# Reordering the pool gate and the key norm inside the mixer of a macaron block

## The chip, the cores and the metric

The kernel runs on one core of a Trainium2 chip. The metric is the device time of one execution in microseconds, and the figure given for a kernel is the median of several runs. For the kernel before, that is 2142.58 us over three runs (2141.94 to 2145.56).

Five engines take part: TensorE (PE) multiplies matrices, VectorE (DVE), ScalarE (ACT) and GpSimd (POOL) do the elementwise work, and SyncE (SP) issues most of the transfers from memory. Each engine works through its own list of instructions in order, and waits on semaphores where it needs what another engine or a transfer makes.

## The reference

The block takes 256 tokens of width 2048 in float32 through a feed-forward part, a mixer and a second feed-forward part (width 5632). The change lies in the mixer alone:

```python
def _hybrid_mixer(u, w_in, ...):
    p = u @ w_in
    z_a, z_b, g_a, g_b = jnp.split(p, IN_SPLITS, axis=-1)   # 3360, 1024, 2048, 2048
    y_a = _rwkv7_branch(z_a, ...) @ w_proj_a
    y_b = _pool_branch(z_b, pool_w, pool_scale) @ w_proj_b
    m = jax.nn.sigmoid(g_a) * y_a + jax.nn.sigmoid(g_b) * y_b
    return m @ w_out

def _rwkv7_branch(z, mu, w0, w2, a0, a2, g2, k_k, k_a, r_k, gn_w, gn_b):
    zs = zf + (_token_shift(zf) - zf) * mu.astype(f32)
    r, k, v, lw, la, lg = jnp.split(zs, RWKV_SPLITS, axis=-1)
    w = -jax.nn.softplus(-(w0.astype(f32) + jnp.tanh(lw) @ w2.astype(f32))) - 0.5
    decay = jnp.exp(-jnp.exp(w))
    a = jax.nn.sigmoid(a0.astype(f32) + la @ a2.astype(f32))
    ...
    kk = hv(k * k_k.astype(f32))
    kk = kk / jnp.maximum(jnp.sqrt(jnp.sum(kk * kk, axis=-1, keepdims=True)), L2_EPS)
    k = k * (1.0 + (a - 1.0) * k_a.astype(f32))
    y = _wkv7_scan(r_h, hv(decay), k_h, v_h, -kk, kk * a_h)
    ...

def _pool_branch(z, pool_w, pool_scale):
    ...                       # per group of 256 columns: mean over the last 2, 4, 8, 16
    mixed = pooled - zf       # tokens, less the token itself
    y = jnp.einsum('bsgc,gcd->bsgd', mixed, pool_w.astype(jnp.float32))
    y = y.reshape(bsz, seq, POOL_WIDTH) * pool_scale.astype(jnp.float32)
```

So a gate multiplies each branch's projection; the pool branch has four groups with a small matrix each (256 by 256), and the recurrent branch needs, per head of 64 columns, the norm of the scaled keys k times k_k.

## The kernel before, in words

**How float32 is multiplied.** Each matrix is held as a high and a low half. A 512 KB piece of weights is loaded into a buffer `w32` (4 of them), ACT copies its high half to `wH` (line 101) and DVE subtracts that to get `wL` (line 102), 5 buffers each. TensorE then does three matmuls per product: high by high, high by low, low by high (`mm3`, or the inner loop of `ch_g`). Nearly all of PE's work is of this kind, and each piece of weights is used once.

**Two shapes of projection.** `tok_g` has tokens on the partitions and 512 output columns: one weight load of four k steps, 24 matmuls of 512 columns. `ch_g` has channels on the partitions: matmuls of 256 columns (line 204). Both are generators: after each three matmuls they yield the time that these are reckoned to take (MM and MC, 0.2265 and 0.12 us each), and on the last one they emit the evacuation of the accumulators.

**The order of the work.** The order of PE's instructions inside the mixer is written out by hand (`manual_schedule`, line 570); the other engines' lists are made by a scheduler that orders ready instructions by priority, where the weight splits and the evacuations of projections get a boost. The hand-made order is:

1. the small projection for decay, a and g (`ch_g`, 288 columns);
2. `z_g(0)`: k, v and r of the first half of the heads, each shifted by one token in `shift`;
3. `p_g`: for each of the four pool groups, the projection `pool_window` (line 587) and, one group late, its mix `pool_mix` (line 621). DVE makes the window sums (3 dependent steps or more per half, line 601 and on) and ACT and DVE split them into `mxT` (lines 616 and 617). The mix of the last group follows directly behind the mix of the third;
4. the recurrent branch, `rwkv` (line 637), for the first and then the second half of the heads. It is a chain of steps with little PE work, and `weave` (line 563) fills the gaps: each `yield 8` in `rwkv` means that 8 us worth of matmuls of the generator `rest()` are put there before the chain goes on. `rest()` (line 551) runs, in order, the pool's projections with their gates, `b_g(0)` to `b_g(2)`; `z_g(1)`, which the second half needs; `b_g(3)`; the four gates `ga_g` of the recurrent branch; and the first part of its projection.

`b_g(c)` computes 512 columns of the pool gate (a `tok_g` over w_in with a sigmoid, into `sgb`) and then the pool's projection (a `tok_g` over w_proj_b, whose operands are the four mixes' results `yb`, listed in `pT`), multiplies the two on DVE, and stores the product to memory through POOL's queue (line 514). The gate for c = 0 was made ahead of the whole mixer (`sgb0`).

**The chain of one half in `rwkv`.** Fifteen registers `R` of 128 by 1024 are made once and shared by both halves; a register's next use waits for its last readers. The steps up to the first products:

- 4 us of fill; the low-rank matmuls `lora` for the decay and for a (16 matmuls), with sigmoids on ACT into registers 0 and 2;
- the running sums of the decay on DVE (16 scans, line 690) into register 4, and the two exponentials on ACT (lines 694 and 695) into 0 and 1;
- v copied with its halves exchanged (register 10), and transposed on PE in two parts, 3 us of fill ahead of each (`pV`, line 718), evacuated by ACT;
- `kk`, four scalings of k on ACT (line 729, register 3), and their square `sq` on ACT (line 730, register 4); 3 us of fill; the norm, 16 small matmuls into `pn` (line 735);
- DVE's lower bound `n1`, the power -0.5 on POOL (`n2`, line 740), and DVE's copy `nb` to 64 columns per head (line 742, register 4 again); 8 us of fill;
- 8 transposes of `nb` into `pk` (line 750), which DVE multiplies into `kk`;
- `k2`, four activations on ACT (line 757) and a DVE multiply (register 5), then the scaled operands `BK` and `AR` on DVE (lines 764 to 787);
- 16 us of fill, the products `pA` (line 800), and further the solve on DVE (lines 837 to 855) with 42 us of fill until `pM` (line 866), the state's recurrence over four chunks, and the output.

The evacuations into PSUM banks go by two pools of four banks: `mm` and `mc` of the projections share one, all the chain's small products share the other.

Of the kernel before, what the change touches and what calls it, by code (L numbers as in the profile page):

```python
# [11 lines left out]
AF = mybir.ActivationFunctionType  # L12
ALU = mybir.AluOpType
# [3 lines left out]
P = 128  # L17
D = 2048
S = 256
DFF = 5632  # L20
NKD = D // P
# [24 lines left out]
class Block:  # L46
# [380 lines left out]
    def mixer(s, prm, uT, rs, resid, emit, gpost, reload):  # L427
        nc = s.nc
        w_in = prm["w_in"]
        at = s.T_at(uT)  # L430
        s.rsb = s.const([P, S], "rsb")

        sgb0 = s.unit((P, 2, 512), F32, "sgb0")

        def ev_sig(dst):
            def ev(h, ps):
                nc.scalar.activation(out=dst(h), in_=ps, func=AF.Sigmoid, scale=rs[h])
            return ev
        GA, GB = RCOLS + W, RCOLS + W + D
        s.gemm_tok(w_in, GB, at, NKD, ev_sig(lambda h: sgb0[:, h]), lead=True)  # L440

        for h in range(2):
            t = s.tmp("rb")
            nc.vector.tensor_copy(t[:, :P], rs[h].to_broadcast([P, P]))
            ps = s.psum("rb")
# [37 lines left out]
        z = [{}, {}]  # L483

        def z_g(hf):
            for nme, zc in (("k", 1), ("v", 2), ("r", 0)):
                z[hf][nme] = s.unit((P, 4, S), F32, "z" + nme)
                for b in range(2):
                    c0 = zc * W + hf * 512 + b * 256

                    def ev_z(banks):
                        s.shift(banks[0], P, c0 // P,
                                [z[hf][nme][:, b * 2 + i] for i in range(2)])
                    yield from s.ch_g(w_in, c0, 256, at, NKD, ev_z, 8)
# [7 lines left out]
            return pT[k // 2][0][:, k % 2], pT[k // 2][1][:, k % 2]  # L502
        msp = s.dp.tile([4, P, 2, 512], F32, tag="msp", name="msp")

        def b_g(c):
            if c == 0:
                sg = [sgb0[:, 0], sgb0[:, 1]]
            else:
                sg = [s.tmp("sgb"), s.tmp("sgb")]
                yield from s.tok_g(w_in, GB + c * 512, at, NKD, ev_sig(lambda h: sg[h]))  # L510

            def ev_pb(h, ps):
                nc.vector.tensor_tensor(out=sg[h], in0=ps, in1=sg[h], op=ALU.mult)
                nc.gpsimd.dma_start(out=msp[c, :, h], in_=sg[h])
            yield from s.tok_g(prm["w_proj_b"], c * 512, at_b, NKW, ev_pb)

        def p_g():
            mix = None
            for g, win in enumerate(POOL_WINDOWS):
                mxT = s.unit((P, 2, 2, S), F32R, "mxT")  # L520
                yield from s.pool_window(g, win, at, w_in, mxT)
                if g:
                    yield from s.pool_mix(g - 1, mix, prm["pool_w"], pT)
                mix = mxT
            yield from s.pool_mix(3, mix, prm["pool_w"], pT)

        sga = []
# [21 lines left out]
        pair = s.pair_g(prm["w_proj_a"], (0, 512), at_a, NKW, 4, (ev_pa(0), ev_pa(1)))  # L549

        def rest():
            for c in range(3):
                yield from b_g(c)
            yield from z_g(1)
            yield from b_g(3)
            for c in range(4):
                yield from ga_g(c)
            for t in pair:
                if t is None:
                    return  # L560
                yield t
# [8 lines left out]
        with s.tc.manual_schedule(engines={mybir.EngineType.PE}):  # L570
            for _ in s.ch_g(w_in, 3 * W, 288, at, NKD, ev_l, 4):
                pass
            for g in (z_g(0), p_g()):
                for _ in g:
                    pass
            fill = rest()
            for hf in range(2):
                weave(chain(hf), fill)
            for _ in fill:
                pass  # L580
# [56 lines left out]
    def rwkv(s, hf, z, lz, prm, yH, yL):  # L637
        nc = s.nc
        V, A, G, T = nc.vector, nc.scalar, nc.gpsimd, nc.tensor
        col = lambda nme, i: s.col[nme][:, hf * 4 + i:hf * 4 + i + 1]  # L640
# [4 lines left out]
        def reg(n, *shape):  # L645
            t = s.R[n]
            if len(shape) == 2:
                return t.rearrange("p (a b) -> p a b", a=shape[0])
            if len(shape) == 3:
                return t.rearrange("p (a b c) -> p a b c", a=shape[0], b=shape[1])  # L650
            if len(shape) == 4:
                return t.rearrange("p (a b c d) -> p a b c d", a=shape[0], b=shape[1],
                                   c=shape[2])
            return t
        ch = lambda t: t.rearrange("p i (c t) -> p i c t", c=NCH)
        fl = lambda t: t.rearrange("p i t -> p (i t)")
# [9 lines left out]
        def lora(ps, n, q):  # L666
            for i in range(2):
                o = cs(2 * q + i)
                T.matmul(ps[:, i], lwH[:, n, o], lz[n], start=True, stop=False)
                T.matmul(ps[:, i], lwL[:, n, o], lz[n], start=False, stop=True)  # L670
        sw = reg(0, 4, S)
        yield 4
        for q in range(2):
            ps = s.psum("pw").rearrange("p (i t) -> p i t", i=2)
# [4 lines left out]
        a = reg(2, 4, S)  # L679
        for q in range(2):  # L680
            ps = s.psum("pa").rearrange("p (i t) -> p i t", i=2)
# [21 lines left out]
        Xd = s.R[4][:, :512].rearrange("p (t g) -> p t g", g=16)  # L703
        Xo = s.R[4][:, 512:].rearrange("p (g t) -> p g t", g=16)
        BKt = [reg(1, *t5), reg(2, *t5)]

        k, v = z["k"], z["v"]
        vs = reg(10, 4, S)
        vp = lambda t: t.rearrange("p i (a b t) -> p (i a) b t", a=2, b=2)
        for b in range(2):  # L710
# [1 line left out]
        for pr in range(2):  # L712
            yield 3
            pss = []
            for src in (v, vs):
                ps = s.psum("pV").rearrange("p (i c) -> p i c", i=4)
# [3 lines left out]
            for b in range(2):  # L720
                c = 2 * pr + b
                pe, po = pss[1 - b], pss[b]
                A.copy(EVs[O, :, c], pe[O, :, :64])
                A.copy(ODs[E, :, c], po[E, :, 64:])

        kk = reg(3, 4, S)
        sq = reg(4, 4, S)
        for i in range(4):
            A.activation(out=kk[:, i], in_=k[:, i], func=AF.Copy, scale=col("k_k", i))
        A.activation(out=fl(sq), in_=fl(kk), func=AF.Square)  # L730
        yield 3
        ps = s.psum("pn")
        for i in range(4):
            for h in range(2):
                T.matmul(ps[:, h * 8 + 2 * i:h * 8 + 2 * i + 2], sq[:, i, h * P:h * P + P],
                         s.bones[:, 0:P:64], start=True, stop=True)
        n1 = s.small(16, "n1", bufs=1)
        V.tensor_scalar(out=n1, in0=ps[:, :16], scalar1=1e-24, scalar2=None, op0=ALU.max)
        n2 = s.small(16, "n2", bufs=1)
        G.tensor_tensor(out=n2, in0=n1, in1=s.mhalf, op=ALU.pow)  # L740
        nb = reg(4, 16, 64)
        V.tensor_copy(nb, n2.unsqueeze(2).to_broadcast([P, 16, 64]))
        nbf = nb.rearrange("p a b -> p (a b)")
        yield 8
        for q in range(2):
            ps = s.psum("pk").rearrange("p (i t) -> p i t", i=2)
            for i in range(2):
                for h in range(2):
# [3 lines left out]
                            op=ALU.mult)  # L752
# [11 lines left out]
        for i in range(4):  # L764
            V.scalar_tensor_tensor(out=qb[:, i], in0=r[:, i], scalar=col("r_k", i),
                                   in1=k2[:, i], op0=ALU.mult, op1=ALU.mult)
# [24 lines left out]
        for q in range(2):  # L791
            ar, bk = AR[q], BK[q]
            for i in range(2):
                g4 = slice(8 * q + 4 * i, 8 * q + 4 * i + 4)
                yield ((16, 0), (3, 4))[q][i]
                pAs = [s.psum("pA").rearrange("p (c j t) -> p c j t", c=NCH, j=2)
                       for _ in range(2)]
                for c in range(NCH):
                    for h, R in ((0, E), (1, O)):
                        T.matmul(pAs[h][:, c], bk[R, i, c], ar[h][R, i, c], start=True,  # L800
                                 stop=True)
                for h, R, RK in ((0, E, O), (1, O, E)):
                    ps = pAs[h]
                    for o in (0, 32):
                        A.copy(Xd[h * 64 + o:h * 64 + o + 32, :, g4]
                               .rearrange("p t g -> p g t"),
                               ps[h * 64 + o:h * 64 + o + 32, :, 0, o:o + 32])
                    A.copy(Xo[h * 64:h * 64 + 32, g4], ps[h * 64:h * 64 + 32, :, 0, 32:])
                    V.tensor_tensor(out=Xrb[R, g4], in0=ps[R, :, 1],
                                    in1=mb[R, :, 1].to_broadcast([64, NCH, C]), op=ALU.mult)  # L810
                    V.tensor_tensor(out=ar[h][RK, i], in0=ps[RK],
                                    in1=mb[RK].to_broadcast([64, NCH, 2, C]), op=ALU.mult)
            yield (5, 4)[q]
            pBs = [s.psum("pB").rearrange("p (i c t) -> p i c t", i=2, c=NCH)
                   for _ in range(2)]
            for i in range(2):
                for c in range(NCH):
                    for h, R in ((0, E), (1, O)):
                        T.transpose(pBs[h][:, i, c],
                                    bk[R, i, c].rearrange("p j t -> p (j t)"),  # L820
                                    s.ident[R, R])
            for h in range(2):
                A.copy(BKt[q][:, :, :, h], pBs[h])
# [35 lines left out]
            A.copy(tt[R, :, o:o + 32], td[R])  # L859
        for h in range(2):  # L860
            G.memset(tt[h * 64 + 32:h * 64 + 64, :, :32], 0.0)
        yield 42
        ps = s.psum("pM").rearrange("p (g t) -> p g t", g=16)
        for g in range(16):
            for h in range(2):
# [95 lines left out]
        for q in range(2):  # L961
            pg = pgs[q]
# [114 lines left out]
```

## Time and profile before

| what | value |
| --- | --- |
| median of three runs | 2142.58 us |
| the profiled execution | 2143.21 us, of which the span is 2141.5 |
| PE busy | 2101.6 us, 11077 matmuls |
| DVE, ACT, POOL busy | 1258.7, 1116.1, 78.1 us |
| memory | 406.99 MB moved, mean 190 GB/s |
| weight splits on DVE (`wL`) | 734, 884.4 us, 1212 ns each |
| weight splits on ACT (`wH`) | 734, 760.1 us, 1042 ns each |
| granted clock of PE over the span | 0.991 |
| PE's share of the chain that ended last | 95% |

The profile comes from one execution. An engine's busy time is what its instructions took; its idle time is put down to what released the instruction that came next. The groups of instructions are listed by line of the kernel, engine and operands; for 128x1024 pieces the splits are the largest groups on DVE and ACT. PE's matmuls overlap in its pipeline, so the mean duration of one (392 ns for 512 columns) is longer than the step from one start to the next. The granted clock is the share of full speed at which PE was allowed to run in a stretch of time; a stage that waited may also show a lower clock behind the wait. The names on the left of an arrow are what is written, those on the right what is read.

### The profile page before, as it was taken

What the parts mean: (1) busy time and instruction counts of PE and PEld (TensorE: products, weight loads), DVE (VectorE), ACT (ScalarE), POOL (GpSimd) and SP (SyncE); (2) the same over time, 40 slices, a digit from 0 to 9 for tenths busy, and PEclk for the clock granted to TensorE, in tenths of its full rate; (3) what the DMA queues carried; (4) which work ended last, traced back from release to release, by engine and by line L of the source; (5) the groups of instructions that cost most, each with busy time, mean ns of one, the idle gap of its engine ahead of it and who ended that gap; (6) DMA issues with size and microseconds to landing.
All of it is one profiled execution on the core that took longest, in us unless ns stands there. A gap on an engine that the chain in (4) does not pass through costs nothing.

```text
span 2141.5 us, 28817 instructions
## 1 busy us (share of the span) xinstructions
PE 2101.6 (98%) x11077; PEld 1769.2 (83%) x11077; DVE 1258.7 (59%) x1588; ACT 1116.1 (52%) x1600; POOL 78.1 (4%) x169
## 2 busy tenths in 40 slices
PE   8999999999999999989999999999999999999998
PEld 6888888888888799978988888878888888888886
DVE  5556555555444555788778666565555555554444
ACT  6565555655444454455465444465565556554442
POOL 1000000000000100010200110010000000000000
PEclk9999999999999999999999999999999999999999
DMA  7656666567666656546545565666666665776664
GB/s 234 191 185 202 194 194 196 180 215 245 191 193 196 205 152 187 171 141 193 143 125 170 167 241 190 194 189 197 193 181 205 195 191 177 219 243 195 195 191 136
DMA packets 223604, 406.99 MB, mean 190 GB/s; under 512 B 13151, under 2 KB 49129, under 8 KB 223465
## 3 DMA queue, kind: packets, MB, share of 16 engines
q1 hardware_dynamic: 216937, 383.11, 58.7%
q0 software_dynamic: 6528, 22.02, 2.9%
q8 instruction: 87, 1.43, 0.3%
q14 instruction: 52, 0.43, 0.1%
HBM read 396.69 MB, written 8.39 MB: 189 GB/s over the span
## 4 chain that ended last, share of the span: by engine, by line
PE 95%; ACT 2%; DVE 2%; issue 1%; DMA 1%; POOL 0%; DVEq 0%; POOLq 0%; SPq 0%; ACTq 0%
PE mm L119 28%; PE mm L120 27%; PE mm L121 27%; PE mc L204 9%; ACT wH L101 1%; DMA w<-in_ffn_gate_dram 1%; DVE wL L102 0%; PE tr L234 0%; PE pA L800 0%; DVE fg L335 0%; PE pU L896 0%; ACT junk L267 0%; PE pSa L908 0%; PE pY L931 0%; PE pY L927 0%
## 5 line engine op out<-in xcount | busy, mean ns | idle before, releaser
L102 DVE TENSOR_TENSOR wL<-w,wH 128x1024 fp32r<-128x1024 f32 (+2 forms) x734 | 884.4, 1212 | 777.1 <-ACT wH L101 775.3
L101 ACT CAST wH<-w 128x1024 fp32r<-128x1024 f32 (+2 forms) x734 | 760.1, 1042 | 872.4 <-PE mm L121 727.2
L119 PE MATMUL mm<-wH,xH 128*128 128x512 f32 x2496 | 977.8, 392 | 6.6 <-ACT xH L240 6.5
L121 PE MATMUL mm<-wH,xL 128*128 128x512 f32 x2496 | 974.8, 391 | 5.2 <-DVE xL L241 5.2
L120 PE MATMUL mm<-wL,xH 128*128 128x512 f32 x2496 | 973.3, 391 | 0.1
L119 PEld LDWEIGHTS mm<-wH,xH 128*128 128x128 f32 x2496 | 470.1, 188 | 107.1 <-ACT xH L240 9.6
L121 PEld LDWEIGHTS mm<-wH,xL 128*128 128x128 f32 x2496 | 469.9, 188 | 104.4 <-DVE xL L241 6.8
L120 PEld LDWEIGHTS mm<-wL,xH 128*128 128x128 f32 x2496 | 470.3, 188 | 97.0 <-DVE wL L102 0.6
L204 PE MATMUL mc<-xH,wH 128*128 128x256 f32 x560 | 161.2, 288 | 0.0
L204 PE MATMUL mc<-xL,wH 128*128 128x256 f32 x560 | 159.2, 284 | 0.0
L204 PE MATMUL mc<-xH,wL 128*128 128x256 f32 x560 | 159.2, 284 | 0.0
L260 ACT COPY x<-T 32x256 f32<-32x256 f32 x352 | 141.8, 403 | 3.9
L204 PEld LDWEIGHTS mc<-xH,wH 128*128 128x128 f32 x560 | 106.7, 191 | 1.2
L204 PEld LDWEIGHTS mc<-xH,wL 128*128 128x128 f32 x560 | 106.7, 191 | 0.2
L204 PEld LDWEIGHTS mc<-xL,wH 128*128 128x128 f32 x560 | 106.7, 191 | 0.2
L279 ACT ACTIVATE sg<-mm,rs 128x512 f32<-128x512 f32 x44 | 30.1, 690 | 20.1 <-PE mm L121 20.1
L280 DVE SCALAR_TENSOR_TENSOR sg<-mm,rs,sg 128x512 f32<-128x512 f32 x44 | 31.6, 751 | 11.9 <-ACT sg L279 11.9
L311 POOL DMA_DIRECT2D gb<-in_ln_ffn_post_dram x4 | 2.2, 562 | 925.6 <-DVE xL L264 892.3
L267 ACT ACTIVATE junk<-mm 128x512 bf16<-128x512 f32 x24 | 14.3, 595 | 34.5 <-PE mm L121 34.5
L314 DVE TENSOR_TENSOR fg<-mm,gb 128x512 f32<-128x512 f32 x24 | 16.5, 692 | 24.5 <-ACT junk L267 24.5
L285 DVE SCALAR_TENSOR_TENSOR sg<-mm,rs,sg 128x512 f32<-128x512 f32 x44 | 30.9, 743 | 0.0
L250 DVE STREAM_TRANSPOSE T<-sg 128x512 f32<-128x512 f32 x44 | 30.9, 701 | 0.0
(236 smaller groups left out, 1016.9 us busy)
## 6 DMA issues: line engine op xcount, KB each, us to landing
w<-in_ffn_up_dram SPq DMA_DIRECT2D x176, 512.0 KB
w<-in_ffn_down_dram SPq DMA_DIRECT2D x176, 512.0 KB
w<-in_ffn_gate_dram SPq DMA_DIRECT2D x174, 512.0 KB
w<-in_w_in_dram SPq DMA_DIRECT2D x128, 512.0 KB
w<-in_w_out_dram SPq DMA_DIRECT2D x32, 512.0 KB
w<-in_w_proj_b_dram SPq DMA_DIRECT2D x16, 512.0 KB
w<-in_w_proj_a_dram SPq DMA_DIRECT2D x16, 512.0 KB
hsp<-fg POOLq DMA_DIRECT2D x16, 256.0 KB, 4.7
```

The source lines that it names most:

```text
L101: nc.scalar.copy(vH, v)
L102: nc.vector.tensor_tensor(out=vL, in0=v, in1=vH.bitcast(F32), op=ALU.subtract)
L119: nc.tensor.matmul(ps, aH, bH, start=start, stop=False)
L120: nc.tensor.matmul(ps, aH, bL, start=False, stop=False)
L121: nc.tensor.matmul(ps, aL, bH, start=False, stop=stop)
L204: s.nc.tensor.matmul(o, lh, rh, start=one and n == 0, stop=k == KT - 1 and n == 2, skip_group_check=True)
L250: s.nc.vector.transpose(out=T1[:, h * 512:h * 512 + 512], in_=src)
L260: nc.scalar.copy(dst[q * 32:q * 32 + 32, :, :, i], src[i * 32:i * 32 + 32, :, :, q])
L279: nc.scalar.activation(out=sg, in_=ps, func=AF.Sigmoid, scale=rs[h])
L280: nc.vector.scalar_tensor_tensor(out=sg, in0=ps, scalar=rs[h], in1=sg, op0=ALU.mult, op1=ALU.mult)
L285: nc.vector.scalar_tensor_tensor(out=sig[h], in0=ps, scalar=rs[h], in1=sig[h], op0=ALU.mult, op1=ALU.mult)
L314: nc.vector.tensor_tensor(out=cc_(fg[h], c), in0=ps, in1=cc_(gb, c), op=ALU.mult)
```

## The change

Two things are reordered. In the pool branch, `b_g` is split into the gate, `gb_g`, and the projection, `pb_g`. The gate of the second 512 columns is now run between the third mix and the last one: `p_g` stops at a `yield None` behind the third mix, the hand-made order runs it only that far, and `rest()` begins with the remainder of `p_g` (the gate, then the last mix), so that these become fill for the first half's chain. The projections 0 and 1 follow, then `z_g(1)`, and the gates and projections 2 and 3.

In `rwkv`, the scaled keys and their square are computed on ACT at the start of the chain, ahead of the low-rank matmuls; the square takes register 5 in place of 4. The norm's matmuls, its power and its copy come ahead of the transposes of v, and the copy `nb` takes register 9 in place of 4. The amounts of fill change accordingly: 4, 2.5, 3, 3, 5.5 in place of 4, 3, 3, 3, 8; and 18 in place of 16 ahead of the first `pA`, 44 in place of 42 ahead of `pM`. The computation is the same.

```diff
-        def b_g(c):
-            if c == 0:
-                sg = [sgb0[:, 0], sgb0[:, 1]]
-            else:
-                sg = [s.tmp("sgb"), s.tmp("sgb")]
-                yield from s.tok_g(w_in, GB + c * 512, at, NKD, ev_sig(lambda h: sg[h]))
+        sgb = {0: [sgb0[:, 0], sgb0[:, 1]]}
+
+        def gb_g(c):
+            sg = sgb[c] = [s.tmp("sgb"), s.tmp("sgb")]
+            yield from s.tok_g(w_in, GB + c * 512, at, NKD, ev_sig(lambda h: sg[h]))
+
+        def pb_g(c):
+            sg = sgb[c]
...
                 mix = mxT
+            yield None
+            yield from gb_g(1)
             yield from s.pool_mix(3, mix, prm["pool_w"], pT)
...
         def rest():
-            for c in range(3):
-                yield from b_g(c)
+            yield from pg
+            yield from pb_g(0)
+            yield from pb_g(1)
             yield from z_g(1)
-            yield from b_g(3)
+            yield from gb_g(2)
+            yield from pb_g(2)
+            yield from gb_g(3)
+            yield from pb_g(3)
...
-            for g in (z_g(0), p_g()):
+            pg = p_g()
+            for g in (z_g(0), iter(pg.__next__, None)):
...
+        k, v = z["k"], z["v"]
+
+        kk = reg(3, 4, S)
+        sq = reg(5, 4, S)
+        for i in range(4):
+            A.activation(out=kk[:, i], in_=k[:, i], func=AF.Copy, scale=col("k_k", i))
+        A.activation(out=fl(sq), in_=fl(kk), func=AF.Square)
         sw = reg(0, 4, S)
         yield 4
...
         BKt = [reg(1, *t5), reg(2, *t5)]
-
-        k, v = z["k"], z["v"]
+        yield 2.5
+        ps = s.psum("pn")
+        for i in range(4):
+            for h in range(2):
+                T.matmul(ps[:, h * 8 + 2 * i:h * 8 + 2 * i + 2], sq[:, i, h * P:h * P + P],
+                         s.bones[:, 0:P:64], start=True, stop=True)
+        n1 = s.small(16, "n1", bufs=1)
+        V.tensor_scalar(out=n1, in0=ps[:, :16], scalar1=1e-24, scalar2=None, op0=ALU.max)
+        n2 = s.small(16, "n2", bufs=1)
+        G.tensor_tensor(out=n2, in0=n1, in1=s.mhalf, op=ALU.pow)
+        nb = reg(9, 16, 64)
+        V.tensor_copy(nb, n2.unsqueeze(2).to_broadcast([P, 16, 64]))
+        nbf = nb.rearrange("p a b -> p (a b)")
+
         vs = reg(10, 4, S)
...
-        kk = reg(3, 4, S)
-        sq = reg(4, 4, S)
-        for i in range(4):
-            A.activation(out=kk[:, i], in_=k[:, i], func=AF.Copy, scale=col("k_k", i))
-        A.activation(out=fl(sq), in_=fl(kk), func=AF.Square)
-        yield 3
...
-        nb = reg(4, 16, 64)
...
-        yield 8
+        yield 5.5
         for q in range(2):
             ps = s.psum("pk").rearrange("p (i t) -> p i t", i=2)
...
-                yield ((16, 0), (3, 4))[q][i]
+                yield ((18, 0), (3, 4))[q][i]
...
-        yield 42
+        yield 44
         ps = s.psum("pM").rearrange("p (g t) -> p g t", g=16)
```

More of the change, by code (lines that the diff above doesn't have):

```diff
@@ L724, in rwkv @@
                 A.copy(ODs[E, :, c], po[E, :, 64:])
-        kk = reg(3, 4, S)
-        sq = reg(4, 4, S)
-        for i in range(4):
-            A.activation(out=kk[:, i], in_=k[:, i], func=AF.Copy, scale=col("k_k", i))
-        A.activation(out=fl(sq), in_=fl(kk), func=AF.Square)
-        yield 3
[L732 to L740, printed above, removed]
-        nb = reg(4, 16, 64)
-        V.tensor_copy(nb, n2.unsqueeze(2).to_broadcast([P, 16, 64]))
-        nbf = nb.rearrange("p a b -> p (a b)")
-        yield 8
+        yield 5.5
         for q in range(2):
```

## The prediction

> **What bounds the kernel now.** I read the page's header first, then who TensorE (PE) waited for in 700 to 1300 us, where the mixer lies, then the stages around those waits with their granted clock, then the timelines of PE, ACT and DVE there.
>
> ```profile
> span 2141.5 us, 28817 instructions
> PE 2101.6 (98%) x11077; PEld 1769.2 (83%) x11077; DVE 1258.7 (59%) x1588; ACT 1116.1 (52%) x1600; POOL 78.1 (4%) x169
> ...
> PE mc L204 <- ACT mxT L616: 5.8, 2, 5.4
> PE pn L735 <- ACT R L730: 4.4, 2, 3.7
> ...
> PE pk L750 <- DVE R L742: 2.2, 1, 2.2
> ...
> 905.00:921.00 16.00, 10.22 (x45) 8.73 (x44) 11.53 (x27) 5.51 (x10) 0.00 (x0) 0.68 0.43 119
> 921.00:944.50 23.50, 22.84 (x124) 19.35 (x124) 19.29 (x39) 18.87 (x33) 1.71 (x3) 1.00 0.45 133
> 944.50:950.00 5.50, 3.26 (x19) 2.55 (x19) 4.16 (x6) 0.86 (x1) 3.17 (x1) 1.00 0.78 243
> 1104.00:1120.00 16.00, 12.29 (x61) 11.49 (x61) 11.04 (x17) 8.82 (x18) 2.90 (x1) 0.68 0.32 97
> ...
> 912.92 0.58 PE L204 MATMUL mc<-mxT,wH 128*128 128x256 f32 x1 [5.39 <-ACT mxT L616]
> ...
> 1106.10 0.28 PE L204 MATMUL mc<-xL,wH 128*128 128x256 f32 x1
> 1110.09 3.58 PE L735 MATMUL pn<-bones,R 128*128 128x2 f32 x16 [3.71 <-ACT R L730]
> ```
>
> PE is busy 98% of the span, so only what PE loses counts. Of the wait rows shown (total, times, longest) three belong to work that the change moves: the pool's last mix (mxT), the key norm (pn) and its transposes back (pk). In the stage rows, the number ahead of the DMA share is the granted clock: 0.68 after the 5.4 and the 3.7 wait, 1.00 after the 2.2 one. So the two long waits cost twice: PE stands, then runs at half clock.
>
> **What the change can remove.** Matmuls follow each other at 0.227 us (512 columns) and 0.12 us (256) at full clock, by the timeline's starts.
> - Mix: 907.25 to 912.92 is 5.67, less one pitch of 0.12: 5.55. The second half waits 0.39. From 912.92 to 920.83 PE runs 12 small and 10 large matmuls, worth 1.44 + 2.27 = 3.71, in 7.91 less the 0.39: 3.81 lost to the clock.
> - Norm of the first head half: 935.70 to 936.75, less 0.23: 0.82. Its pk: 945.92 to 948.55, less 0.23: 2.40.
> - Norm of the second half: 1106.10 to 1110.09, less 0.12: 3.87. From 1110.09 to 1118.89 PE does 16 norm matmuls (1.81 where they ran at full clock), 15 small and 5 large ones with 0.1 of switching, worth 4.8, in 8.8: 4.0 lost.
>
> Sum 5.55 + 0.39 + 3.81 + 0.82 + 2.40 + 3.87 + 4.0 = 20.8 us. PE's instructions are the same in number; only their order differs.
>
> **The gate ahead of the last mix.** In the changed order PE goes from the third mix at 905.93 to 18 gate matmuls (4.09), the lora (1.91), 12 gate (2.75), norm (1.88), 12 (2.73), v transposes (0.9), 15 (3.4), transposes (0.9), 24 (5.45), pk (0.9), 15 (3.4). With the third mix (1.44) that puts the last mix at 935.7, against 907.4 now. Its operand needs the window sums that DVE ends at 914.3 today. In the new order DVE threads them between scans and splits; counted through DVE's list the last of them is ready at 931.3, and the mix's weights at 931.9. So the 5.55, the 0.39 and the 3.81 go, with 3.8 us to spare. SP issues the same loads in another order: eight gate loads come ahead of the pool's 256 KB one. A load took 2.7 us from the free buffer to its last packet when nothing else ran; the tightest I find (the last split of the first projection) has 5 us. POOL's queue now has the norm's power ahead of the first two stores, which nobody waits for before the end of the mixer.
>
> **Norm earlier.** The square moves to before the decay, so ACT has it long before the norm. For the second half it must wait for the first half's last transposes, whose source it overwrites; they start at T. ACT's four scalings start T+1.1 and take 1.9, the square 0.95: T+4.0. The norm on PE follows after 2.35 of transposes, 18 large matmuls 4.1, lora 1.9, 12 large 2.7: T+11.1. Slack 7, so 3.87 and 4.0 go. pk in the second half had no wait. In the first half the norm reaches DVE at 919.9; POOL's power takes 3.8 (3775 ns here, 2902 in the other half) and DVE's copy 0.7: 925.0, against pk at 931.4. Slack 6, so 0.82 and 2.40 go. The square now sits in the register of the new keys (k2), so ACT's four k2 activations wait for the norm matmuls, done 918.0; ACT reaches them at 921.1, so that wait is free. One more table load (1.28) is not on this path.
>
> **What is late next.** The mix's evacuation. Its last piece (yb, second low half) stands on DVE behind the first half's keys: from the k2 multiply, which waits for ACT until 923.2, DVE's list up to it is: k2 1.26, broadcast 0.65, eight weight splits of 1.15 and a half one of 0.6, r times r_k 1.58, k2 and r scalings 2.83 + 0.61 + 0.65, kk multiplies 1.2, the block of a, b and kk 4.28, b scalings 2.83, yb pieces 3 x 0.4 and the mix operand 0.33. That is 27.3 us: done 950.5. PE comes to the matmul that needs it after the mix at 935.7 + 1.44, 36 matmuls of the projection (8.2) and 8 more (1.8): 947.2. A new wait of 3.3 us. Bounds: 0, if DVE is 3.3 us earlier (12% of its list); 9.3, if DVE idles in it as in 921 to 944.5 (busy 19.29 of 23.5). I take 3.3, since nothing in the list waits for PE or a load by my count.
>
> Does the clock fall in it? The 2.2 us wait left it at 1.00, the 3.7 one did not, and 3.3 is nearer to that. The mean of 0.63 in 1108 to 1110 puts the fall at 1108.5, 2.1 us after PE's last matmul ended. I take a fall. Rows for its price: 3.8 and 4.0 above; and after the first FFN, 746.59 to 750.14 has 8 large matmuls in 3.55 instead of 1.82: 1.7. The mean of the three is 3.2; ends 0 and 4.0.
>
> [...]
>
> After this, by the same walk: the solve of the first half (DVE, 40.6 us from 988.3 to 1028.9, with pM 5.5 us later) gets about 3.3 us more shift work and 2 more us of cover. The second half's weight splits run 1.7 us or more ahead. I cost both at nothing; a solve late by more than the 4.2 left would show as a wait of pM, us for us.
>
> **Sum.** The profiled execution took 2143.2 us (span 2141.5); the median of the three runs is 2142.6, 0.6 lower. 2143.2 - 20.8 + 3.3 + 3.2 = 2128.9, less 0.6: 2128.3 us, 0.67% faster. A measurement tells about 0.2%, 4.3 us, from no change.
>
> **The rivals.**
> 1. The wait is there but the clock holds: 2125.1. [...]
> 2. DVE is early, no new wait: 2121.8. It needs 12% off DVE's list, all of it from rows of this trace.
> 3. The second half's norm waits as before (the change does not do there what it says, because the square still needs the old register): 2128.3 + 7.9 = 2136.2. Against it the 7 us of slack; for it that ACT is in order, and a late transposes' evacuation or split ahead of the square moves it.
> 4. DVE becomes the bound of the first half: the evacuation sits behind in-order key work that waits for ACT. If DVE were busy there only 59%, its mean over the span, 27.3 us take 46.3, the mark is 969.5, PE waits 22.3 and loses 4.0: 2142.6 - 20.8 + 26.3 = 2148.1, slower. It decides from a mark of about 965 (no gain) and 969 (slower). Against it: DVE is busy 82% in 921 to 944.5, and would have to wait 19 us in work whose inputs I find ready.
>
> **How the numbers follow.** Forecast 45%, its own range 2125 to 2132 (wait 2 to 5, clock 1.7 to 4.0). Rival 1 20%, rival 2 9%, rival 3 10%, rival 4 10%; 6% for a DVE mark between 960 and 968 that ends within 0.2%. The range takes in 2 and 3: 2121 to 2137, 84%. Faster 0.84, same 0.06, slower 0.10.
>
> **What would show it.** No wait of mc for mxT, of pn for the square, of pk for the broadcast; clock 1.00 from 905 to 945 and after the second half's norm. One wait near 947 of a projection matmul on DVE's yb, 2 to 5 us, with the clock at 0.5 behind it. DVE busy almost without a break for 27 us ahead of it. The forecast is wrong if that wait is over 9 us, if pn waits again in the second half, or if pM or pA begin to wait.

## The result, and the profile after

The changed kernel takes 2126.68 us (median of four runs, 2124.88 to 2128.84) against 2142.26 for the kernel before in the same comparison. The ratio is 0.9924, with a 95% interval from 0.9907 to 0.9942: faster by 0.8%. The forecast was 2128.3, in a range of 2121 to 2137.

The page's header of the changed kernel, its line of busy times, and the waits of PE from 700 to 1300 us (engine, line, tile waited for: total, times, longest):

```profile
span 2124.2 us, 28823 instructions
PE 2093.8 (99%) x11077; PEld 1762.0 (83%) x11077; DVE 1257.3 (59%) x1588; ACT 1115.9 (53%) x1600; POOL 77.7 (4%) x169
...
PE mm L121 <- DVE yb L639: 3.2, 1, 3.2
PE mm L121 <- DVE xL L241: 2.4, 1, 2.4
PE mm L119 <- ACT xH L240: 2.0, 2, 1.5
PE pS L925 <- ACT R L919: 0.9, 1, 0.9
```

The three waits that the change was to remove (mxT, the square for pn, the copy for pk) are gone, and one has come: a projection matmul that waits 3.2 us for DVE's yb. The wait of pS has grown from 0.2 to 0.9.

The stages of the changed kernel that answer to those shown of before (stretch, length, busy time of PE, its weight loads, DVE, ACT and POOL, granted clock, DMA share, GB/s):

```profile
905.00:921.00 16.00, 16.00 (x98) 14.16 (x98) 15.41 (x43) 12.84 (x21) 1.84 (x1) 1.00 0.53 155
921.00:944.50 23.50, 23.50 (x119) 19.84 (x118) 22.31 (x36) 16.72 (x30) 1.63 (x2) 1.00 0.42 138
...
1104.00:1120.00 16.00, 16.00 (x72) 13.27 (x71) 15.80 (x25) 5.78 (x8) 1.69 (x3) 1.00 0.72 224
```

PE is busy through all of them at full clock, where before it was busy 10.22 and 12.29 of 16 at 0.68 in the first and last. DVE is busier in the same stretches, 15.41 instead of 11.53 in the first.

The new wait, in the timelines of PE and of DVE (start, duration, instruction, and in brackets the idle time and what ended it):

```profile
945.99 0.39 PE L120 MATMUL mm<-wL,yb 128*128 128x512 f32 x1
949.57 0.50 PE L121 MATMUL mm<-wH,yb 128*128 128x512 f32 x1 [3.19 <-DVE yb L639]
...
922.34 1.23 DVE L768 TENSOR_TENSOR R<-R,zk 128x1024 f32<-128x1024 f32 x1 [0.93 <-ACT R L766]
...
943.94 2.78 DVE L785 TENSOR_TENSOR R<-R,R 64x512 f32<-64x512 f32 x4
946.76 2.36 DVE L102 TENSOR_TENSOR wL<-w,wH 128x1024 fp32r<-128x1024 f32 x2
949.03 0.48 DVE L639 SCALAR_TENSOR_TENSOR yb<-mc,cols,yb 128x256 fp32r<-128x256 f32 x1
```

From the start of the k2 multiply (922.34) to the end of the last yb (949.51) DVE takes 27.2 us. The prediction's list of this stretch came to 27.3.

**Where the time went.** From the first matmul of the mixer's small projection to the output transposes of the second half's chain (pT), PE takes 491.3 us before (770.70 to 1261.95) and 475.6 after (769.87 to 1245.50). So 15.6 us of the 17.3 by which the spans differ lie in this stretch, where the change is; it is called the mixer's stretch below. The removed terms, 20.8, less the new wait (945.99 to 949.57 is 3.58, less a pitch of 0.23: 3.35) and one stretch of 3.41 us at half clock behind it (1.7) give 15.75. That they meet so closely is partly luck: the 0.7 us that pS waits more isn't among them. The other 1.7 us lie outside the change, in equal parts ahead of it and behind it.

### The profile page after: what moved, and what is told of

Its sections match the earlier page's. It is cut to its first block, busy times and chain, and to the rows that moved or that the text cites. A ratio compares the mean times of both kernels' runs of the same rounds, so it can differ in the third digit from the quotient of the medians.

```text
span 2124.2 us, 28823 instructions
## 1 busy us (share of the span) xinstructions
PE 2093.8 (99%) x11077; PEld 1762.0 (83%) x11077; DVE 1257.3 (59%) x1588; ACT 1115.9 (53%) x1600; POOL 77.7 (4%) x169
## 4 chain that ended last, share of the span: by engine, by line
PE 95%; DVE 2%; issue 1%; ACT 1%; DMA 1%; SPq 0%; DVEq 0%; POOLq 0%; POOL 0%; ACTq 0%
PE mm L119 28%; PE mm L121 27%; PE mm L120 27%; PE mc L204 10%; DVE wL L102 1%; DMA w<-in_ffn_gate_dram 1%; DVE fg L335 0%; PE pA L809 0%; PE tr L234 0%; ACT wH L101 0%; PE pU L905 0%; PE pY L940 0%; PE pSa L917 0%; DMA w<-in_w_proj_b_dram 0%; ACT junk L267 0%
```

## Experiments

The theory: each of the three old waits is lost time together with the clock behind it, the gate's order removes the first, the early square and norm the others, and the new wait is a matter of order on DVE alone. Rivals: one part carries all; the parts need each other; the new wait is held by something other than DVE's list.

### The gate's order alone

The changed kernel with `rwkv` as it was before:

```diff
-        sq = reg(5, 4, S)
...
-        A.activation(out=fl(sq), in_=fl(kk), func=AF.Square)
         sw = reg(0, 4, S)
...
-        yield 2.5
-        ps = s.psum("pn")
...
-        yield 5.5
+        sq = reg(4, 4, S)
...
+        A.activation(out=fl(sq), in_=fl(kk), func=AF.Square)
+        yield 3
+        ps = s.psum("pn")
...
+        nb = reg(4, 16, 64)
...
+        yield 8
...
```

> The gate ahead of the last mix alone, with the keys, the square and the norm as they were before. My theory, by the prediction's terms: the mix's wait and its clock (5.55 + 0.39 + 3.81 = 9.75 us) go, the norm's four terms (0.82, 2.40, 3.87, 4.0) stay, and the new wait for yb of 3.2 us with a cold window of some 1.8 comes with the gate order: 2142.3 - 9.75 + 5.0 = 2137.5 us; 2132.5 if the norm's own waits leave DVE the time so that yb is not late. A wait of pn of about 3.9 us in the second half, none of the mix for mxT. The rival, that the gate's order carries the whole change: 2127 us.

Measured: 2139.03 us, ratio 0.9981 (0.9972 to 0.9989) to 2142.53. Of the waits of PE from 700 to 1300 us the longest, and the instruction that waited:

```profile
PE pn L744 <- ACT R L739: 7.2, 2, 4.0
...
928.18 3.15 PE L744 MATMUL pn<-bones,R 128*128 128x2 f32 x14 [3.99 <-ACT R L739]
```

The mix's wait is gone, and so is the first half's wait of pk, which was to stay; the second half's pn still waits, 3.2 us. The size is near, but that is luck, as the reason that I gave for the cost is wrong: no wait for yb came. In its place the first half's norm waits 3.99 where it waited 0.66 before. The gate order brings PE to the norm at 924 instead of 936, and ACT has the square only when it has done decay, exponentials and the copies of v. PE loses those 4 us and runs 10.24 us at half clock (927.46 to 937.70, last section), and by the time it comes to yb, yb is there. So a gain of 9.75 at the mix gave only 3.5.

### The keys and the norm alone

The kernel before with the changed `rwkv`; `b_g`, `p_g` and `rest` as they were:

```diff
+        sq = reg(5, 4, S)
...
+        A.activation(out=fl(sq), in_=fl(kk), func=AF.Square)
         sw = reg(0, 4, S)
...
+        yield 2.5
+        ps = s.psum("pn")
...
+        nb = reg(9, 16, 64)
...
         vs = reg(10, 4, S)
...
-        sq = reg(4, 4, S)
...
-        ps = s.psum("pn")
...
-        nb = reg(4, 16, 64)
...
```

> The keys and the square early and the norm ahead of the transposes of v, with the gate order as it was before. My theory: the norm's terms go (0.82 + 2.40 + 3.87 + 4.0 = 11.1), the mix's wait of 5.4 us and its clock stay, and no wait for yb is seen, since the mix comes before the keys: 2142.3 - 11.1 = 2131.2 us (2129 to 2134). The rival, that the parts need each other (the early keys push the mix's window sums back on DVE): a longer wait for mxT, 2135 us or more.

Measured: 2132.03 us, ratio 0.9951 (0.9939 to 0.9964). PE's waits from 900 to 1300 us:

```profile
PE mc L204 <- ACT mxT L616: 5.8, 2, 5.4
PE pB L819 <- DVE R L811: 0.6, 1, 0.6
```

As expected: 10.5 us gained against 11.1 in the sum, the mix's wait unchanged at 5.4, no wait for yb. The early keys did not push the mix's window sums back.

In the mixer's stretch the gate's order alone gains 5.9 us (to 485.3) and the keys and the norm alone 9.6 (to 481.6), together 15.5 of the change's 15.6. So in time the parts simply add, and the gate's order gives about 6 us with the early square as without it. What the square changes is where PE is stopped: without it at the norm, with it at yb.

### The square early, the norm in its old place

```diff
-        yield 2.5
-        ps = s.psum("pn")
...
-        V.tensor_copy(nb, n2.unsqueeze(2).to_broadcast([P, 16, 64]))
...
         vs = reg(10, 4, S)
...
-        yield 5.5
+        yield 3
+        ps = s.psum("pn")
...
+        V.tensor_copy(nb, n2.unsqueeze(2).to_broadcast([P, 16, 64]))
...
+        yield 8
...
-                yield ((18, 0), (3, 4))[q][i]
+                yield ((16, 0), (3, 4))[q][i]
...
-        yield 44
+        yield 42
```

> The changed kernel with the scaled keys and their square made early as in the change, but the norm's matmuls, its power and its copy back behind the transposes of v, with the old amounts of fill. My theory: it is the early square that takes away the norm's wait in the second half (3.87 and its clock 4.0), so these stay away; in the first half the copy of the norm comes later on DVE and PE waits 1 to 2 us at the transposes pk, while the wait for yb falls by about as much: 2126.7 + 0 to 2 = 2126 to 2129 us. The rival, that the norm's place is what counts: PE waits for the square again in the second half, 2126.7 + 7.9 = 2134.6 us.

Measured: 2131.48 us, ratio 0.9946 (0.9932 to 0.9960) to 2143.92 on that chip. PE's waits from 700 to 1300 us, and DVE in the second half:

```profile
PE pk L758 <- DVE R L750: 5.9, 2, 3.5
...
PE mm L121 <- DVE yb L639: 0.6, 1, 0.6
...
1100.11 0.17 DVE L746 TENSOR_SCALAR n<-pn 128x16 f32<-128x16 f32 x1
1100.77 1.23 DVE L767 TENSOR_TENSOR R<-R,zk 128x1024 f32<-128x1024 f32 x1 [0.48 <-ACT R L765]
...
1104.69 2.77 DVE L786 TENSOR_TENSOR R<-R,R 64x512 f32<-64x512 f32 x4
1107.50 1.23 DVE L102 TENSOR_TENSOR wL<-w,wH 128x1024 fp32r<-128x1024 f32 x1
1108.64 0.69 DVE L750 COPY R<-n 128x1024 f32<-128x1024 f32 x1
```

Neither theory gives the whole. pn no longer waits for the square in either half, so the early square alone removes that, as the theory said. But pk now waits 2.4 us in the first half (foreseen) and 3.5 in the second (not foreseen). 8.5 us lie between DVE's n1 and its copy: POOL has the power done at 1103.3, but the copy stands on DVE behind key work and an evacuation (1100.77 to 1107.5) and a weight split. With the norm moved ahead of the transposes, the copy is done at 1094 and pk comes at 1102.6. So the place of the norm counts as well, through DVE's queue and not through the square: the mixer's stretch is 479.9 us here against 475.6 in the changed kernel, 0.2% of the whole. By the ratios alone that is not clear, since their intervals overlap.

### More work on DVE ahead of yb

```diff
         V.tensor_tensor(out=fl(k2), in0=fl(k2), in1=fl(k), op=ALU.mult)
+        for _ in range(3 if hf == 0 else 0):
+            V.tensor_tensor(out=fl(reg(6, 4, S)), in0=fl(k2), in1=fl(k), op=ALU.mult)
```

> The changed kernel with three more multiplies of the size of the k2 multiply (1.26 us each, 3.8 us) on DVE among the first half's keys, ahead of the last yb in its list; their result is overwritten. My theory: DVE has no slack there, so the last yb comes 3.8 us later and PE's wait grows from 3.2 to 7.0 us; with up to one or two more cold windows of 1.7: 2130.5 us, to 2133.9. The rival, that the wait for yb is set by something other than DVE's list (ACT's high half, a load) and DVE has slack: the wait stays at 3.2, 2126.7 us.

Measured: 2130.84 us, ratio 0.9944 (0.9932 to 0.9957). PE's wait for yb, and a short one ahead of it:

```profile
PE mm L121 <- DVE yb L639: 5.9, 1, 5.9
...
945.71 0.50 PE L120 MATMUL mm<-wL,yb 128*128 128x512 f32 x1 [0.24 <-DVE wL L102]
```

The time came out as expected, the wait 1.1 us short of it. The stretch from the k2 multiply (923.02) to the last yb (start 953.1) is 3.4 us longer than in the changed kernel. PE reached its wait 0.7 us later against the start of the mixer, since it had already stopped at 945.71 for a weight split, which stands on the same longer list of DVE. That leaves 2.7. The half clock behind it lasted 6.83 us instead of 3.41, of which 2.3 us still fall into the wait. DVE's list sets this wait nearly us for us.

### Other work ahead of the projection

```diff
             yield from pg
+            zg = z_g(1)
+            yield from itertools.islice(zg, 32)
             yield from pb_g(0)
             yield from pb_g(1)
-            yield from z_g(1)
+            yield from zg
```

> The changed kernel with one block of the second half's k projection (96 matmuls of 256 columns, 11.5 us) placed between the last mix and the projection that reads it. The same work in another order. My theory: the 3.2 us wait for yb is one of order alone, DVE reaches the last yb at the same time and PE comes 11.5 us later: the wait and the cold window behind it go, 2126.7 - 3.35 - 1.8 = 2121.5 us. The rival, that something else holds PE there (the loads of w_proj_b, at a DMA share of about 1.0 around 952 us, or the splits): a wait of the same length for a split, 2126 to 2128 us.

Measured: 2122.79 us, ratio 0.9907 (0.9892 to 0.9922). All that is left of PE's waits from 900 to 1300 us:

```profile
PE pS L927 <- ACT R L921: 0.9, 1, 0.9
```

The wait is gone with no new one in its place, and nothing else held PE there. Beside the changed kernel on one chip:

> The changed kernel once more, on the chip of the two that follow, so that they can be set against it directly. 2126.7 us; the wait for yb of 3.2 us, with one or two windows of 3.4 us at half clock behind it (1.7 us each), by where it falls on their grid.

> The kernel with the k block between the last mix and its projection, beside the changed kernel on one chip. By its first run 3.9 us below the changed kernel; by the terms (wait 3.35, clock 1.9) 5.2 us below. If the gain was a matter of the chip alone: within 2 us of it.

The changed kernel took 2127.42 us (ratio 0.9928, 0.9914 to 0.9942), this one 2122.80 (0.9907, 0.9893 to 0.9920): 4.6 us less, near to the 5.2 of the terms. Each of its runs there (2121.49 to 2123.84) is below each of the changed kernel's (2124.99 to 2128.45), and its mixer's stretch is 470.8 us in both of its profiles, against 475.6 and 474.1. It is the fastest version found without extra work.

### Extra matmuls in the wait

Twelve matmuls whose result nobody reads, directly ahead of the one that waits for yb:

```diff
         nc.tensor.matmul(ps, aH, bL, start=False, stop=False)
+        for _ in range(pad[1]):
+            nc.tensor.matmul(pad[0], aH, bH, start=True, stop=True)
...
+                               12 if c == 0 else 0)
```

> The changed kernel with 12 extra matmuls of 512 columns (2.7 us at full clock, result unused) put on PE directly ahead of the matmul that waits 3.2 us for yb. They prolong nothing if the wait is as long as they are. My theory: what is lost behind the wait is only the clock's fall, which the extra work prevents: a wait of 0.5 us is left, the clock stays at 1.00 from 945 to 960, 2126.7 - 1.9 = 2124.8 us. The rival, that the slower matmuls behind the wait come from something else (loads, the weights of w_proj_b): the clock column or the pace there stays low, 2126.7 us, or 2129 if DVE is no later than PE.

> The kernel with the extra matmuls ahead of the wait for yb, beside the changed kernel on one chip. If the clock's fall costs 1.9 us there: 2 us below the changed kernel, and 3.3 us above the one with the k block. If the slower pace behind the wait has another cause: level with the changed kernel.

Measured: 2123.87 us (ratio 0.9909, 0.9895 to 0.9922), and 2126.59 (0.9922, 0.9909 to 0.9934) on the chip of the repeated runs, 0.8 below the changed kernel there. In both profiles 0.5 us of the wait is left and the clock stays at 1.00 from 945 to 960. The medians decide nothing: they lie further apart than the effect. The profile of the repeated changed kernel shows one reason; there the same wait left the clock up without help:

```profile
944.27:947.68 3.41, 2.11 (x10) 1.42 (x8) 3.34 (x5) 1.04 (x1) 0.00 (x0) 1.00 0.84 262
947.68:951.10 3.42, 1.53 (x7) 1.27 (x8) 3.42 (x5) 0.26 (x1) 0.00 (x0) 1.00 0.58 161
951.10:954.51 3.41, 3.41 (x10) 2.27 (x10) 1.97 (x3) 0.79 (x1) 1.15 (x2) 0.50 1.05 347
```

```profile
944.16:947.57 3.41, 1.74 (x8) 1.12 (x6) 3.35 (x5) 1.04 (x1) 0.00 (x0) 1.00 0.71 228
947.57:950.99 3.42, 1.91 (x8) 1.61 (x9) 3.42 (x5) 0.64 (x1) 0.00 (x0) 1.00 0.71 195
950.99:954.40 3.41, 3.41 (x39) 2.78 (x39) 1.59 (x2) 1.35 (x4) 1.15 (x2) 1.00 1.00 339
```

The first three rows are of the changed kernel's first profile, the others of its second, both in rows of 3.41 us, the first cut by the clock's steps at 951.10 and 954.51. In the first, the wait (about 3.2 us) leaves PE idle for 1.30 us of one row and 1.89 of the next, and the third runs at 0.50. In the second it is shared 1.67 and 1.51, and the third runs at 1.00, with 39 matmuls begun in place of 10.

The mixer's stretch decides what the medians can't. It takes 475.6 us in the first of these profiles and 474.1 in the second, and 474.1 in both profiles with the extra matmuls. So the fall costs 1.6 us where it comes, the extra matmuls save that much and no more, and they gain nothing in a run where the clock would have held.

### Extra matmuls where PE waits longest outside the change

The kernel of the k block, and ten such matmuls ahead of the third matmul of the first projection behind each of the two norms between the parts:

```diff
+            pad = (pss[1], 10) if lead and not first and k == 0 and h == 0 else (None, 0)
             s.mm3(pss[h], xH[:, h * P:h * P + P], xL[:, h * P:h * P + P], wH, wL,
-                  k == 0, k == KT - 1)
+                  k == 0, k == KT - 1, pad)
...
```

> The kernel with the k block between the last mix and its projection (2122.8 us), and the same kind of extra matmuls, 10 of 512 columns, in the two places outside the change where PE waits longest: the first projection behind each of the two norms between the parts, ahead of its third matmul, where PE waits 2.4 us for the low half of the operand. My theory: the clock falls there for one to three windows (in the profiles 3.4 to 10.2 us at 0.5), which cost 1.3 to 3 us at each place; the waits themselves stay. 2122.8 - 4.4 = 2118.4 us (2117 to 2120). The rival, that the clock has fallen by the time the extra matmuls start, or that they end later than the wait: they take up to 4.5 us instead of 2.4, 2123 to 2127 us.

Measured: 2122.25 us, ratio 0.9899 (0.9885 to 0.9912), which can't be told from the version without them. PE in the first of the two places:

```profile
739.02 2.45 PE L122 MATMUL mm<-wH,xH 128*128 128x512 f32 x10
741.55 0.50 PE L123 MATMUL mm<-wH,xL 128*128 128x512 f32 x1
...
747.18 0.79 PE L119 MATMUL mm<-wH,xH 128*128 128x512 f32 x1 [1.41 <-ACT xH L243]
```

The extra work filled the wait of 2.4 us without prolonging it, and the mean clock of the profiled run rose from 0.995 to 0.997. But at this place it only put the fall off: the clock went to one half from 747.0 to 750.4 (its mean is 0.76 from 745 to 752), where full matmuls stand, and without the extra work from 742.7 to 746.1, where PE ran eight transposes and few matmuls. The waits behind did not stay as they were either: PE reaches its next long stop three matmuls further on and waits 1.41 us there, where the next wait for a high half had been 0.52 without it. Matmul against matmul, this profile loses 1.8 us at the first place to the one without extra work. At the second place the clock is at 1.00 from 1382 to 1395, where without it its mean was 0.66 from 1380 to 1395, but a wait of 1.47 us comes in place of 0.53, and 1.3 us are gained. Against the second profile without extra work the loss is 0.5 and the gain 0.9. Why ACT makes that high half no earlier stays open. Of the 4.4 us that I expected, the medians show 0.5 and the ratios 1.7, both within the noise.

## Why the prediction was right, point by point

- **The old waits.** Right. The runs of the parts show two of the sums: 10.5 against 11.1 us for the norm, and the mix's wait and clock gone in every run with the gate's order.
- **The walk of the first half.** Right to a microsecond. The mix was put at 935.7 and starts at 934.79; yb's end at 950.5 and is at 949.51; PE's arrival at 947.2, and it stops behind 945.99. About 0.8 us of each is that this run was that much earlier at the start of the mixer. (A load took longer than the 2.7 us given: in the trace of before the 512 KB issued at 902.86 have their last packet at 906.09, 3.2 us. That is still inside the 5 us, and PE waited for no split there in the changed kernel, by its list from 700 to 1300 us.)
- **The second half's norm** (the rival with 10%). Right to set it aside: the transposes start at 1076.5, the square is done 3.7 us later (4.0 foreseen) and pn starts 10.9 later (11.1). Slack 7.
- **The norm of the first half.** Right: DVE's copy was put at 925.0 and ends at 924.2, pk at 931.4 and starts at 930.5. POOL's power took 2.9 where I had allowed 3.8. (The terms given add up to 924.4, not 925.0, and those of DVE's list to 27.2, not 27.3; neither matters to the forecast.)
- **The new wait.** Right: 3.3 foreseen, 3.2 in both profiles. It needs both parts: neither alone shows it.
- **The clock behind the wait.** The mis-sized term. I took 3.2 us, the mean of three rows, on the ground that 3.3 is nearer to the wait of 3.7, in which the clock fell, than to the one of 2.2, which left it at 1.00. It was 1.6 in one profile and nothing in the other. The ground was wrong, by the trace of before itself: in the first projection behind the norm, ahead of the mixer, the clock fell behind a wait of 2.37 (0.50 from 743.28 to 750.10), and my third row lies just behind it:

```profile
742.07 0.49 PE L121 MATMUL mm<-wH,xL 128*128 128x512 f32 x1 [2.37 <-DVE xL L241]
...
743.00:747.00 4.00, 3.00 (x11) 1.93 (x11) 3.13 (x8) 3.94 (x13) 2.75 (x5) 0.53 1.06 402
```

So in these traces the length of a wait alone doesn't tell whether the clock falls. The two larger rows had other things behind them: a second wait of 0.39 us at the mix, the small matmuls of the norm at pn. At both the clock stood at 0.50 for 10.24 us (910.53 to 920.77, 1108.50 to 1118.74), where behind yb full matmuls follow and it did so for 3.41. And the same wait of 3.2 us had the fall behind it in one profile and none in the other, so my forecast and the first rival (the clock holds, 2125.1) are two cases of one kernel.

- **DVE as the bound** (2148.1). Did not come: DVE was busy 26.8 of the 27.1 us from 922.4 to 949.5, where that rival needed it at 59%.
- **The second half of the mixer, costed at nothing.** Nearly right: pM and pA wait for nothing, but pS waits 0.7 us more.

The sum with the clock at 1.6 instead of 3.2 is 2128.3 - 1.6 = 2126.7, against 2126.68 and 2127.42 measured. That it meets the medians to within 1 us is partly luck, since runs of this one kernel lie between 2124.88 and 2128.84, and its two profiles also differ in the clock at two waits outside the mixer. The mechanism does not rest on it: the waits that went and the one that came are in the traces.

## What to carry to other kernels

When PE is nearly always busy, walk the other engine's list to the point where PE next needs it: a stretch of 27 us on DVE, added up from single durations, gave the new wait to 0.2 us. Whatever lets PE come sooner exposes what the next engine has not yet done, so a removed wait need not pay in full; here the gate's order took away 9.75 us at the mix and gave about 6 in the mixer's stretch, with the early square or without it. A new wait that is purely one of order goes away by placing independent work ahead of it; the late engine need not become faster. And a stretch between two marks on PE, read from the traces, told 1.6 us apart where whole runs of one kernel spread over 4.

## What the runs showed of the hardware

The stretches at half clock lasted 3.41, 6.83 or 10.24 us: in the kernel before 6.83 ahead of the mixer (743.28 to 750.10) and 10.24 at the mix and at pn, in the changed kernel's first profile 3.41 behind yb, with more work on DVE 6.83 there. In the trace of before the clock's steps from 743.28 to 1118.74 lie 6.83, 160.43, 10.24, 187.73 and 10.24 us apart, all of them whole multiples of 3.413. The rows below are of that length.

In the kernel before, the wait of 2.2 us left the clock up, with PE busy for 1.64 of 3.41 us:

```profile
944.67:948.08 3.41, 1.64 (x8) 1.02 (x6) 2.88 (x4) 0.69 (x1) 3.00 (x1) 1.00 0.79 244
948.08:951.49 3.41, 2.94 (x17) 2.63 (x18) 2.59 (x6) 1.05 (x1) 0.00 (x0) 1.00 0.86 302
```

In the changed kernel's first profile the clock fell behind a row in which PE was busy for 1.53 of 3.42 us, and in its second it did not behind rows with 1.74 of 3.41 and 1.91 of 3.42. PE's ends are modelled, so these numbers are rough, and what decides on a fall is not shown by so few rows.

In the changed kernel's first profile the clock came back behind a row in which PE had no idle time (3.41 of 3.41 from 951.10). In the gate's order alone the second row here has none either, and the third is still at 0.50; pn's small matmuls run there from 928.18 to 931.33. Behind the third, from 937.70 to 941.12, the clock is at 1.00:

```profile
927.46:930.88 3.42, 2.70 (x13) 2.70 (x13) 3.36 (x6) 1.61 (x2) 0.00 (x0) 0.50 0.00 0
930.88:934.29 3.41, 3.41 (x11) 2.87 (x11) 1.47 (x3) 0.00 (x0) 1.79 (x1) 0.50 0.86 259
934.29:937.70 3.41, 3.41 (x9) 2.64 (x8) 0.69 (x1) 0.57 (x1) 1.15 (x1) 0.50 0.55 202
```

The spread of a kernel's own runs goes with the clock: those of the changed kernel at 2124.88 and 2125.91 us have a mean granted clock of 0.995, the one at 2128.84 has 0.993, and 0.002 of its span is 4.3 us. What makes this difference is not shown, as only one run of each set was profiled.
